# A planned attention-and-convolution layer on one core: fewer dummy transpositions at the opening, and another computed order of work

## The chip, the cores and the metric

The kernel runs on one core of one Trainium2 chip. The metric is the device time of one execution in microseconds (us). A core has TensorE (PE in the profile; PEld is its loading of weights), VectorE (DVE), ScalarE (ACT), GpSimd (POOL) and SyncE (SP). SP and POOL here issue DMAs; each of the engines works through its own list of instructions in order, so an instruction that waits holds back everything behind it on that engine.

## The reference

One decoder layer on x of 1024 tokens by 1024 channels. The numbers in brackets are column ranges of one input projection of 5632 columns.

```python
h = rmsnorm(x, norm_g)
proj = einsum('bsd,de->bse', h, w_in)                     # 1024 x 5632
q, k, v, a_gate, c_val, c_glu, c_gate = split(proj)       # 1024, 256, 256, 1024, 1024, 1024, 1024
y_att  = attention_branch(q, k, v, a_gate)     # 16 query heads, 4 key heads, three dilated windows
                                               # mixed by softmax denominators; times silu(a_gate)
y_conv = conv_branch(c_val, c_glu, c_gate, ...)  # val*sigmoid(glu), 31-tap causal convolution per
                                                 # channel, layernorm over channels, silu, silu(gate)
x = x + einsum('bse,ed->bsd', concat(y_att, y_conv), w_out)
return rmsnorm(x, final_norm_g)
```

## The kernel before

Nothing in this kernel is issued in the order in which it is written. The functions below `layer_kernel` only record operations in a list (`Plan.op`), each with an engine, an assumed cost, the buffers that it reads and writes, and a priority, which is its place in the list less the `boost` in force (`TUNE`). `Plan.order` (from L323) then plays the whole list through a clock for each engine. At each step it takes the operation that can start earliest, and of those that can start at once the one with the lowest priority number. The order found is the order of every engine's instructions. For an operation of SP or POOL, which is a DMA, the planned landing is the planned start plus 1.1 us, or the end of the DMA planned before if that is later, plus a time by size, plus 0.9 us (L397). What reads the data can't be planned earlier than that. `LIMITS` says how many buffers of a name may be held at once in the plan: three split weight tiles (`wh`, `wl`), two score tables (`tab`), five convolution inputs (`hc`), and so on. On the chip nothing of the planned times is left, only the order and the true dependencies.

Precision is kept by splitting a float32 operand into a rounded high part and a rest (`split_r`, `split_dma`); a product of two such operands takes three passes (high by high, high by low, low by high). A projection of 128 columns (`inproj`) is therefore 2 halves of 512 tokens x 8 blocks of channels x 3 = 48 matmuls of 128x512.

**The opening** (`prepare`). `pl.mm([...] * WARM)` records transpositions of a constant into a bank that nobody reads (tile `idle`). Then, for eight tiles of 128 tokens: load of `x`, sum of squares, scale (`stt` of x with `r` and with `gbc`, the norm gain spread over partitions by four matmul passes), transposition on TensorE (`xT`), split into `hhi` and `hlo`. Behind the first and the second token tile come `MORE[0]` and `MORE[1]` further dummy transpositions. `parameters` loads the convolution's weights and three vectors into the tile `rows` (the last is `in_ln_b`) and transposes them (`par_ps`).

**The sections.** `SECTIONS` lists which projections are recorded beside which pair of heads. A letter is a kind: h two projections for one convolution input, c a convolution gate, a an attention gate, q, k, v as usual. The number behind the list says how many `attend` go with it. So the first `attend` is in the section "h2 a0 q1", the third, attend(2), in "q3 h4", the last, attend(7), in "c4 c5". Each of the first eight sections also carries one `convolve`. An `attend` is scores on TensorE, a table added on VectorE, an exponential on ScalarE, transpositions back, and products with v.

**Behind the sections** come `load_wo_att` (load `raw_oa`, split into `woah` and `woal`, eight times), `layer_norm` for two halves (matmuls `mean`, `var`, `rb`), the attention part of the output projection (`att_part`: load `ya`, split, 24 matmuls `opsa` for each bank) and then the convolution part (`conv_part`: `yc`, matmuls `opsc`), which ends with the final norm and the stores. `outproj` loads the first `ya` only after the last `woal` has been written (the argument `after`).

Of the kernel before, what the change touches and what calls it, by code (L numbers as in the profile page):

```python
# [31 lines left out]

LIMITS = {"x": 5, "raw": 1, "raw_oc": 1, "raw_oa": 2, "wh": 3, "wl": 3, "tab": 2, "e": 7, "pt": 4, "vs": 4, "vc":
          4, "turn": 2, "opsa": 2, "score": 2, "hc": 5, "c": 7, "t": 1, "g": 1, "gl": 7, "y": 2, "ag": 4, "cc": 5,
          "qs": 5, "qf": 4, "kdh": 9, "kdl": 6, "yc": 2, "ya": 2, "zc": 7, "za": 3}

RESERVE = {"e": 7, "pt": 3}
BANKS = {"mm": 3, "sc": 2, "tp": 2, "o": 1}  # L40
WARM = 55
LATE = C_CG + 6 * P
MORE = (10, 12)
TUNE = {"w": 195, "use": 240, "ln": 65, "att": 240, "conv": 5, "wo": 215, "woa": -20, "ap": 0, "wait": 0.2116}
SECTIONS = [("k0 q0 h1 v", 0), ("h2 a0 q1", 1), ("h3 a1 q2 a2", 1), ("q3 h4", 1), ("h5 k1 a3 q4", 1), ("h6 a4 q5",
            1), ("c0 h7 a5 q6", 1), ("c1 q7 a6 a7 c2 c3", 1), ("c4 c5", 1), ("c6 c7", 0)]


def score_tables():
# [112 lines left out]
class Plan:  # L162
# [141 lines left out]
    def order(self):  # L304
# [20 lines left out]
        dma, table = 0.0, None  # L325
# [34 lines left out]
        while len(out) < n:  # L360
            best = None
            for e, todo in ready.items():
                now, pick = None, None
                for i in sorted(todo, key=self.prio.__getitem__):
                    t = start_of(i)
                    if t is None:
                        continue
                    soon = t - TUNE["wait"] if self.prio[i] < i - 300 else t
                    if now is None or soon < now - 1e-9:
                        now, pick, start = soon, i, t  # L370
                        if soon <= clock[e]:
                            break
                if pick is not None and (best is None or start < best[0]):
                    best = (start, pick)
            if best is None:
                raise RuntimeError(f"no slots: {oldest}, {inuse}, { {k: len(f) for k, f in free.items()} }, "
                                   f"{[(i, [b.name for b in ops[i][4]]) for r in ready.values() for i in sorted(r)[:3]]}")
            t, i = best
            e, cost, _, _, bufs = ops[i]
            if i in self.tables and self.tables[i] != table:  # L380
                table = self.tables[i]
                cost += 1.3
            ready[e].remove(i)
            for b in bufs:
                if not b.fixed and b not in held:
                    held.add(b)
                    if b.group:
                        inuse[b.group] = inuse.get(b.group, 0) + 1
                        taken[b.group] = taken.get(b.group, 0) + 1
                    b.slot = min(free[b.kind])[1]  # L390
                    free[b.kind].remove(min(free[b.kind]))
            end = t + cost
            clock[e] = end
            done = end + self.LATENCY
            if e in ("SP", "POOL"):
                dma = max(dma, t + 1.1) + self.dma_time[i]
                done = dma + 0.9  # L397
            elif e == "DVE":
                done = end + 0.13
            for b in bufs:  # L400
                if b.kind in PSUM_KINDS:
                    bank[b] = (e, done)
            same = {"PE": end, "ACT": end + 0.03}.get(e, done)
            for u in users[i]:
                at[u] = max(at[u], same if ops[u][0] == e else done)
                need[u] -= 1
                if not need[u]:
                    ready[ops[u][0]].append(u)
            for b in bufs:
                left[b] -= 1  # L410
                if not left[b] and not b.fixed:
                    free[b.kind].append((done, b.slot))
                    if b.group:
                        inuse[b.group] -= 1
            self.when[i] = t
            out.append(i)
            done_ops[i] = True
            while oldest < n and done_ops[oldest]:
                oldest += 1
# [44 lines left out]
def layer_kernel(tc, x, norm_g, w_in, conv_w, conv_b, ln_g, ln_b, w_out, fin_g, tab, out):  # L464
# [3 lines left out]
    def pool(name, space=None):  # L468
# [7 lines left out]
        **{k: (ps, k, BANKS[k]) for k in PSUM_KINDS},  # L476
    }, LIMITS)

# [34 lines left out]
    def c4(shape, name, dtype=F32):  # L513
        group = name.rstrip("0123456789_")
        return pl.buf("c4", shape, dtype, name, group=group if group in pl.limits else None)

    def bank(kind, name, group=None):
        return pl.buf(kind, [P, 512], F32, name, group=group)
# [12 lines left out]
    def split_r(hi, lo, src):  # L531

        pl.act(hi, src, AF.Copy)
        pl.tt(lo, src, hi.cast(F32), ALU.subtract)
# [12 lines left out]
    idle = bank("o", "idle")  # L547
    pl.mm([(idle[:, 0:P], ident, ident, None, None)] * WARM)
    rows = c4([P, D], "rows")
# [6 lines left out]
    def prepare(half):  # L556
# [12 lines left out]
        for j in range(4):  # L569
# [18 lines left out]
            for cg in range(2):  # L588
# [5 lines left out]
                split_r(hhi[half][:, 4 * cg:4 * cg + 4, o:o + P], hlo[half][:, 4 * cg:4 * cg + 4, o:o + P], b.split(P))  # L594
            if tb < len(MORE):
                pl.mm([(idle[:, 0:P], ident, ident, None, None)] * MORE[tb])
            for k in sorted(first_w) if tb == 1 else ():
# [25 lines left out]
    def load_raw(col):  # L623
        raw = c4([P, ND, P], f"raw{col}")
        pl.load(raw, w_in[:, col:col + P].rearrange("(c p) n -> p c n", p=P))
        return raw

    def split_w(col, raw, split=split_dma):
        wh, wl = c4([P, ND, P], f"wh{col}", F32R), c4([P, ND, P], f"wl{col}", F32R)
        split(wh, wl, raw)  # L630
        return wh, wl

    def load_w(col):
        if col in ready:
            return ready[col]
        old, pl.boost = pl.boost, TUNE["w"]
        w = split_w(col, load_raw(col), split_r if col >= LATE else split_dma)
# [3 lines left out]
    def inproj(col, use, cuts=((0, 512), (0, 512))):  # L641
        wh, wl = load_w(col)
        for half in range(2):
            b = bank("mm", f"ps{col}_{half}")
            for n0, n1 in zip(cuts[half], cuts[half][1:]):
# [5 lines left out]
                for c in range(0, ND, 2):  # L651
                    pl.mm([(b[:, n0:n1], wl[:, c + i, :], hhi[half][:, c + i, n0:n1], False, c + i == ND - 1)
                           for i in range(2)])
            pl.boost = TUNE["use"]
            use(half, b, slice(half * 512, half * 512 + 512))
# [448 lines left out]
    def boosted(name, gen):  # L1104
        while True:
            pl.boost = TUNE[name]
            w = next(gen, None)
            pl.boost = 0
            if w is None:
                return  # L1110
            yield w

    def section(k, weight, spine, more=()):
        nonlocal done
        proj, m = SECTIONS[k]
        hs = [boosted("att", attend(i)) for i in range(done, done + m)]
# [48 lines left out]
```

## Time and profile before

| | us |
|---|---|
| median of 3 runs | 899.86 (898.11 to 900.07) |
| the profiled execution, its own time | 898.14 |
| span of the profiled execution, first to last instruction | 896.3 |
| TensorE busy | 873.2 |
| VectorE busy | 655.8 |
| ScalarE busy | 592.8 |

The span lacks 1.84 us of the execution's own time, which lie around it. A busy TensorE is not one at its peak, since matmuls overlap in the profile: a 128x512 matmul is shown with some 0.39 us and starts 0.23 us behind the one before it. So idle time, the granted clock and the starts tell more than the busy share.

### The profile page before, as it was taken

How to read it: one execution, taken by the hardware profiler on the slowest of the kernel's cores; microseconds unless marked ns; L12 is line 12 of the kernel's file. 1: busy time of each engine (PE TensorE's matmuls, PEld its weight loads, DVE VectorE, ACT ScalarE, POOL GpSimd, SP SyncE). 2: the span in 40 equal slices, each digit the busy share in tenths (PEclk: the TensorE clock that was granted, in tenths of full speed). 3: DMA queues.
4: the chain of work that ended last, by engine and by line, in shares of the span. 5: the costliest groups of instructions: out<-in, count | busy, mean ns of one | idle time of the engine just before them, and what ended most of it. 6: DMA issues, size and time to landing. Idle time of an engine off the chain costs nothing.

```text
span 896.3 us, 13046 instructions
## 1 busy us (share of the span) xinstructions
PE 873.2 (97%) x4493; PEld 720.2 (80%) x4493; DVE 655.8 (73%) x1506; ACT 592.8 (66%) x1392; POOL 53.3 (6%) x69
## 2 busy tenths in 40 slices
PE   8999999999999999999999999999999799999996
PEld 7888888888888788887887887888787678878885
DVE  5769996689699689789989779943649895625333
ACT  4777368677958867977977947983896744414111
POOL 0001001010010010010010110101000000000000
PEclk9999999999999999999999999999999799999999
DMA  7533607254553474545355744455773697777111
GB/s 266 164 71 58 153 3 165 50 116 77 138 111 81 100 150 108 139 71 143 78 112 143 165 94 130 89 137 112 217 261 141 204 363 238 252 217 229 71 48 47
DMA packets 104953, 123.53 MB, mean 138 GB/s; under 512 B 17941, under 2 KB 78357, under 8 KB 104888
## 3 DMA queue, kind: packets, MB, share of 16 engines
q1 hardware_dynamic: 97000, 94.40, 34.3%
q0 software_dynamic: 7888, 28.32, 17.9%
q8 instruction: 35, 0.57, 0.3%
q14 instruction: 30, 0.25, 0.1%
HBM read 65.35 MB, written 24.84 MB: 101 GB/s over the span
## 4 chain that ended last, share of the span: by engine, by line
PE 86%; DMA 7%; DVE 3%; ACT 2%; issue 1%; SPq 1%; POOL 0%; DVEq 0%; ACTq 0%; POOLq 0%
PE ps L237 52%; PE opsc L237 10%; PE opsa L237 7%; PE sc_near L237 3%; PE on L237 3%; PE of L237 3%; PE sc_far L237 2%; DMA y<-comb 2%; PE tp_p L235 1%; PE tp_m L235 1%; DMA rows<-in_ln_b 1%; PE tp_s L235 1%; DMA raw_oc<-in_w_out 1%; ACT e L252 1%; DMA yc<-yc_dram 1%; DMA x<-in_x 1%
## 5 line engine op out<-in xcount | busy, mean ns | idle before, releaser
L237 PE MATMUL ps<-hhi,wh 128*128 128x512 f32 (+1 forms) x720 | 288.1, 401 | 0.3 <-ACT hhi L250 0.2
L237 PE MATMUL ps<-hlo,wh 128*128 128x512 f32 (+1 forms) x720 | 279.6, 390 | 0.3 <-DVE hlo L265 0.3
L237 PE MATMUL ps<-hhi,wl 128*128 128x512 f32 (+1 forms) x720 | 188.7, 395 | 0.0
L237 PEld LDWEIGHTS ps<-hhi,wh 128*128 128x128 f32 x720 | 135.6, 188 | 31.4 <-issue 0.5
L237 PEld LDWEIGHTS ps<-hlo,wh 128*128 128x128 f32 x720 | 135.8, 189 | 27.6 <-DVE hlo L265 0.8
L237 PEld LDWEIGHTS ps<-hhi,wl 128*128 128x128 f32 x720 | 129.3, 188 | 27.9
L252 ACT ACTIVATE e<-e,near 128x256 f32<-128x256 f32 (+1 forms) x256 | 115.6, 488 | 22.2 <-DVE near L265 12.3
L269 DVE SCALAR_TENSOR_TENSOR c<-hc,taps,c 128x511 f32<-128x511 f32 (+14 forms) x120 | 88.4, 737 | 0.3
L269 DVE SCALAR_TENSOR_TENSOR c<-t,taps,c 128x511 f32<-128x511 f32 (+14 forms) x120 | 88.6, 738 | 0.0
L269 DVE SCALAR_TENSOR_TENSOR t<-hc,taps,t 128x511 f32<-128x511 f32 (+6 forms) x112 | 82.5, 736 | 0.8 <-ACT t L252 0.8
L237 PE MATMUL opsc<-woc,yhc 128*128 128x512 f32 (+1 forms) x272 | 80.8, 381 | 0.0
L252 ACT ACTIVATE e<-e,far 128x224 f32<-128x224 f32 (+1 forms) x128 | 54.0, 424 | 36.0 <-DVE far L284 35.7
L298 POOL DMA_DIRECT2D wl<-raw x40 | 34.7, 868 | 452.1 <-ACT wl L252 350.1
L237 PEld LDWEIGHTS opsc<-woc,yhc 128*128 128x128 f32 x272 | 50.2, 188 | 10.6
L252 ACT ACTIVATE fjunk<-zc 128x512 bf16<-128x512 f32 (+1 forms) x17 | 10.3, 606 | 68.0 <-DVE zc L265 67.8
L237 PE MATMUL opsc<-woc,ylc 128*128 128x512 f32 (+1 forms) x136 | 52.0, 382 | 1.5 <-DVE ylc L265 1.5
L284 DVE CUSTOM_DVE_ANT_0 e<-sc_near,tab 128x256 f32<-128x256 f32 (+1 forms) x128 | 45.0, 404 | 9.9 <-PE sc_near L237 9.2
L250 ACT CAST wh<-raw 128x1024 fp32r<-128x1024 f32 x44 | 46.0, 1044 | 1.6 <-DMA raw<-in_w_in 1.4
L237 PE MATMUL opsa<-woah,yla 128*128 128x512 f32 x112 | 45.5, 406 | 1.5 <-DVE yla L265 1.5
L237 PE MATMUL opsa<-woah,yha 128*128 128x512 f32 x112 | 45.4, 405 | 0.0
L237 PE MATMUL opsa<-woal,yha 128*128 128x512 f32 x112 | 45.0, 402 | 0.0
L252 ACT ACTIVATE e<-e,f 128x96 f32<-128x96 f32 (+1 forms) x128 | 44.5, 439 | 0.2 <-DMA f<-back 0.2
(166 smaller groups left out, 1405.1 us busy)
## 6 DMA issues: line engine op xcount, KB each, us to landing
raw<-in_w_in SPq DMA_DIRECT2D x44, 512.0 KB, 4.5
wl<-raw POOLq DMA_DIRECT2D x40, 512.0 KB, 4.9
x<-in_x SPq DMA_DIRECT2D x8, 512.0 KB, 8.5
tab<-in_tab SPq DMA_DIRECT2D x8, 512.0 KB, 3.4
c_dram<-c SPq DMA_DIRECT2D x8, 512.0 KB, 3.3
g_dram<-g SPq DMA_DIRECT2D x8, 512.0 KB, 2.8
raw_oa<-in_w_out SPq DMA_DIRECT2D x8, 512.0 KB, 5.7
raw_oc<-in_w_out SPq DMA_DIRECT2D x8, 512.0 KB, 7.4
```

The lines of the kernel that those rows point to most:

```text
L235: nc.tensor.transpose(out.ap(), a.ap(), b.ap())
L237: nc.tensor.matmul(out.ap(), a.ap(), b.ap(), start=start, stop=stop)
L250: nc.scalar.copy(out.ap(), x.ap())
L252: nc.scalar.activation(out.ap(), x.ap(), func, **{k: ap_of(v) for k, v in kw.items()})
L269: lambda: self.nc.vector.scalar_tensor_tensor(out.ap(), a.ap(), ap_of(s), b.ap(), op0, op1),
L284: lambda: self.nc.vector.tensor_tensor_reduce(out.ap(), a.ap(), b.ap(), 1.0, ap_of(first), ALU.add, ALU.min, least.ap()),
L298: self.op("POOL", 1.0, lambda: self.nc.gpsimd.dma_start(ap_of(dst), x.ap(), accum_op=ALU.add), [dst], [x, dst])
```

## The change

The order of all instructions is computed anew, from these edits:

- 26 dummy transpositions in place of 55 at the start; 8 and 8 in place of 10 and 12 behind the first two token tiles.
- The planner takes every DMA's landing to be 1.0 us later (1.9 in place of 0.9).
- Limits: `wh` 4 (was 3), `hc` 7 (5), `qs` 6 (5), `zc` 8 (7); `tab` 1 (2), `cc` 4 (5), `kdl` 5 (6), `yc` 1 (2).
- Boosts: weight loads 215 (195), evictions of projections 120 (240), convolution -105 (5), output weights for the convolution part 155 (215), for the attention part -240 (-20), attention output 20 (0).
- Sections: the projection a2 goes from the section of attend(1) to that of attend(2); c3 goes from the section of attend(6) to that of attend(7); some are listed in another order.

No operation is added, and only dummy transpositions are taken away (29 + 2 + 4 = 35).

```diff
-LIMITS = {"x": 5, "raw": 1, "raw_oc": 1, "raw_oa": 2, "wh": 3, "wl": 3, "tab": 2, "e": 7, "pt": 4, "vs": 4, "vc":
-          4, "turn": 2, "opsa": 2, "score": 2, "hc": 5, "c": 7, "t": 1, "g": 1, "gl": 7, "y": 2, "ag": 4, "cc": 5,
-          "qs": 5, "qf": 4, "kdh": 9, "kdl": 6, "yc": 2, "ya": 2, "zc": 7, "za": 3}
+LIMITS = {"x": 5, "raw": 1, "raw_oc": 1, "raw_oa": 2, "wh": 4, "wl": 3, "tab": 1, "e": 7, "pt": 4, "vs": 4, "vc":
+          4, "turn": 2, "opsa": 2, "score": 2, "hc": 7, "c": 7, "t": 1, "g": 1, "gl": 7, "y": 2, "ag": 4, "cc": 4,
+          "qs": 6, "qf": 4, "kdh": 9, "kdl": 5, "yc": 1, "ya": 2, "zc": 8, "za": 3}
...
-WARM = 55
+WARM = 26
 LATE = C_CG + 6 * P
-MORE = (10, 12)
-TUNE = {"w": 195, "use": 240, "ln": 65, "att": 240, "conv": 5, "wo": 215, "woa": -20, "ap": 0, "wait": 0.2116}
-SECTIONS = [("k0 q0 h1 v", 0), ("h2 a0 q1", 1), ("h3 a1 q2 a2", 1), ("q3 h4", 1), ("h5 k1 a3 q4", 1), ("h6 a4 q5",
-            1), ("c0 h7 a5 q6", 1), ("c1 q7 a6 a7 c2 c3", 1), ("c4 c5", 1), ("c6 c7", 0)]
+MORE = (8, 8)
+TUNE = {"w": 215, "use": 120, "ln": 65, "att": 240, "conv": -105, "wo": 155, "woa": -240, "ap": 20, "wait": 0.2116}
+SECTIONS = [("k0 q0 h1 v", 0), ("h2 a0 q1", 1), ("h3 a1 q2", 1), ("a2 q3 h4", 1), ("h5 k1 a3 q4", 1), ("h6 a4 q5",
+            1), ("c0 h7 a5 q6", 1), ("a6 c1 a7 q7 c2", 1), ("c5 c4 c3", 1), ("c6 c7", 0)]
...
                 dma = max(dma, t + 1.1) + self.dma_time[i]
-                done = dma + 0.9
+                done = dma + 1.9
```

## Rows read from the trace of the kernel before

**Rows 1.** The page's first part: busy time, share and instructions of each engine.

```profile
PE 873.2 (97%) x4493; PEld 720.2 (80%) x4493; DVE 655.8 (73%) x1506; ACT 592.8 (66%) x1392; POOL 53.3 (6%) x69
```

**Rows 2.** Stretches: from:to, length, busy PE, PEld, DVE, ACT, POOL, clock, DMA, GB/s.

```profile
0.00:24.20 24.20, 19.91 (x138) 17.44 (x138) 13.02 (x29) 12.29 (x22) 1.02 (x8) 0.97 0.79 264
24.20:296.00 271.80, 271.80 (x1432) 225.89 (x1433) 225.05 (x534) 196.93 (x478) 20.66 (x24) 1.00 0.44 98
296.00:317.00 21.00, 18.91 (x114) 15.72 (x114) 13.18 (x32) 19.73 (x54) 0.88 (x1) 1.00 0.39 101
692.90:704.30 11.40, 4.96 (x21) 3.37 (x19) 9.21 (x18) 7.72 (x11) 0.00 (x0) 0.75 0.81 261
888.90:896.30 7.40, 0.02 (x1) 0.00 (x0) 1.98 (x7) 1.44 (x4) 0.00 (x0) 0.78 0.19 72
```

**Rows 3.** TensorE's waits: who waited for whom: total us, times, longest.

```profile
PE rb L237 <- DVE lst L269: 4.3, 1, 4.3
PE par_ps L235 <- DMA rows<-in_ln_b: 1.7, 1, 1.7
```

**Rows 4.** Order of time, TensorE, opening: start, us, what, count [idle before <-releaser].

```profile
1.45 8.23 PE L235 MATMUL idle<-ident 128*128 128x128 f32 x55 [1.45 <-POOL ident masks.py:199]
9.61 1.98 PE L237 MATMUL gbc<-gain,avg 1*128 1x512 f32 x4
11.52 1.31 PE L235 MATMUL idle<-ident 128*128 128x128 f32 x10
...
21.54 0.66 PE L235 MATMUL par_ps<-ident,rows 34*128 34x34 f32 x8 [1.70 <-DMA rows<-in_ln_b]
```

**Rows 5.** Order of time, VectorE, opening.

```profile
10.77 2.92 DVE L269 SCALAR_TENSOR_TENSOR x<-x,xst,gbc 128x512 f32<-128x512 f32 x4 [2.42 <-PE gbc L237]
```

**Rows 6.** Chain that ended last, opening: start, us, what.

```profile
9.87 11.42 DMA rows<-in_ln_b
```

**Rows 7.** Stretches of the opening, columns as in rows 2.

```profile
22.00:24.00 2.00, 1.62 (x12) 1.17 (x10) 0.57 (x1) 1.57 (x3) 0.00 (x0) 0.67 0.88 249
24.00:26.00 2.00, 1.82 (x9) 1.82 (x10) 2.00 (x5) 1.50 (x5) 0.00 (x0) 0.50 0.63 180
```

**Rows 8.** Chain, a stretch that TensorE makes alone: start, us, what, matmuls.

```profile
757.73 29.16 PE opsa L237 x126
```

**Rows 9.** Order of time, TensorE, the gap inside 296 to 317.

```profile
311.04 0.33 PE L235 MATMUL tp_w<-ident,e 128*128 128x128 f32 x1 [1.19 <-ACT e L252]
...
316.34 0.51 PE L237 MATMUL ps<-hhi,wh 128*128 128x512 f32 x1
```

**Rows 10.** Order of time, the passage from projections to the output projection: TensorE.

```profile
692.92 1.02 PE L237 MATMUL mean<-csum,avg 128*128 128x512 f32 x2
700.48 2.05 PE L237 MATMUL rb<-ident,lst 128*128 128x128 f32 x8 [4.28 <-DVE lst L269]
704.31 0.80 PE L237 MATMUL opsa<-woah,yla 128*128 128x512 f32 x1 [0.93 <-DVE yla L265]
```

**Rows 11.** The same passage on VectorE and on SP's queue.

```profile
696.31 1.22 DVE L265 TENSOR_TENSOR woal<-raw_oa,woah 128x1024 fp32r<-128x1024 f32 x1
703.17 1.09 DVE L265 TENSOR_TENSOR yla<-ya,yha 128x896 fp32r<-128x896 f32 x1
697.60 0.45 SPq L295 DMA_DIRECT2D ya<-y_dram  x1
```

**Rows 12.** A stretch of 20 us ahead of that passage, columns as in rows 2.

```profile
660.00:680.00 20.00, 20.00 (x118) 16.62 (x117) 13.83 (x22) 16.57 (x37) 0.00 (x0) 1.00 0.48 176
```

**Rows 13.** DMA issues: out<-in, queue, count, KB each, median us from issue to landing.

```profile
raw<-in_w_in SPq DMA_DIRECT2D x44, 512.0 KB, 4.5
raw_oc<-in_w_out SPq DMA_DIRECT2D x8, 512.0 KB, 7.4
ya<-y_dram SPq DMA_DIRECT2D x8, 448.0 KB, 7.9
yc<-yc_dram SPq DMA_DIRECT2D x8, 512.0 KB, 7.1
```

## The prediction

> **What bounds the kernel now.** I read the busy shares first, then the span cut into stretches, then TensorE's waits, then the order of time at each place where TensorE stood still. TensorE is busy 97% of the span [rows 1], VectorE and ScalarE about 70%. The stretches tell more [rows 2]: from 24.2 to 296 us TensorE has not one idle moment, at a clock of 1.00. What it loses lies in few places: 4.3 us idle of the first 24.2; 2.1 idle between 296 and 317; 6.4 idle of the 11.4 us from 692.9 to 704.3, with a clock of 0.75; and the last 7.4, in which it has nothing left to do. These are 20 of its 23 idle us (896.3 less 873.2). TensorE's longest wait, 4.3 us, is that of `rb`, layer norm's broadcast, for VectorE; next comes the parameters' transposition, 1.7 us for a DMA [rows 3]. The work of TensorE is the same before and after, dummies apart. So the change can gain where TensorE stands still or runs slow, and nowhere else; it can lose anywhere, since a new order can open a gap inside the 272 us that have none.
>
> **The opening, fewer dummies.** The 55 transpositions run from 1.45 to 9.68, 0.150 us each on average, and the four passes of `gbc` stand behind them [rows 4]. VectorE had the first scale factors at 8.35 and then waited 2.42 us for `gbc` [rows 5]. With 26, at 0.150 each, the dummies end at 5.4. Ten later ones took 1.31 us, 0.13 each [rows 4]; if all 26 ran at half that speed, 0.26 each, they end at 8.2. Both lie ahead of 8.35. `gbc` takes 1.98 us and its first half serves the first operation on VectorE, so VectorE starts at 8.35 to 9.2, that is 1.6 to 2.4 us earlier than at 10.77. No row shows when the gain's DMA landed, only that it had by 9.61; if that is the bound, the shift is smaller, down to none. The six dummies taken from behind the token tiles are hidden by VectorE's scaling, which takes 2.92 us for the two tiles [rows 5]; they are put at nothing, and 6 x 0.13 = 0.8 if uncovered.
>
> What is late next decides how much survives. At 19.84 TensorE reached the parameters' transposition and stood until 21.54 for the load of `in_ln_b`, which took 11.42 us from 9.87 on [rows 4, 6]. Nothing in the change makes that load faster. If the order stays, TensorE only arrives there earlier and waits longer: gain zero. If the transposition falls behind the next token tiles, the gain is the 2.4, the 1.7 and the low clock that followed: 0.67 for two us and 0.50 for two [rows 7] lost 0.7 + 1.0. So the ends are 5.8 gained and 1.7 lost (a longer wait and once more such a spell of low clock). The planner moves the landing of x and of the parameters by the same 1.0 us, so their order may well stay; I take 1.5 gained, nearer to zero.
>
> On the clock: it fell to 0.50, the lower of its two levels (1.2 of 2.4 GHz), after TensorE had stood still from 19.84 to 21.54 [rows 4, 7]. The Trainium skill (TensorE: Matmul & The Clock Gate, Part 1) says that the low clock is the default and that only activity lifts it. That speaks against taking dummies away; it is worked out from rows as a rival below.
>
> **A projection moved beside attend(2).** A 128x512 matmul takes 29.16 / 126 = 0.2314 us [rows 8], so a projection of 48 is 11.1 us of TensorE. Between 309 and 316 TensorE had none left and ran at the pace of the softmax: it waited 1.19 us for ScalarE at 311, and the next projection began at 316.34 [rows 9], in a stretch with ScalarE busy 19.73 of 21 [rows 2]. That is attend(2), whose section has three projections' worth of columns; a2 makes it four, at the cost of the section before, which has no idle to 296. A fourth `wh` buffer also lets the weights be ready sooner. The gain is at most the 2.1 idle, at least 0; I take 1.8.
>
> **A projection moved beside attend(7), and the passage to the output projection.** After its last projection TensorE does `mean` at 692.9, waits 4.28 for `rb`, starts `opsa` at 704.3 and runs the first of them at a low clock [rows 2, 10]. The chain behind it: the last `woal` is written at 697.53, the load of `ya` leaves at 697.60, and `yla` is ready at 704.26 [rows 11]. So `opsa` hangs on the weight splits. With c3 moved, 11.1 us of TensorE work no longer stand ahead of attend(7), so attend(7) can begin and end some 11 us earlier, and its followers on ScalarE and VectorE with it. VectorE has room: 13.8 us busy of 20 from 660 to 680 [rows 12]. Against it stands the boost of the splits, which falls by 220 places. For no gap at all the last `woal` must be written about as early as `ya` (7.9 median [rows 13]) and its two splits (0.94 + 1.09, of which only the second has its row [rows 11]; the first is put at the same 1.1) take: 10 us ahead of the last projection's end at 693, that is at 683, 14 us earlier than now. Ends: 8 gained (6.4 idle, and for the clock 1.6 of the 11.4 x 0.25 = 2.9 that it lacks, since part of that fell into idle time anyway), 8 lost (the gap once more). I take 3 gained, the priority and the section pulling against each other.
>
> **Later landings.** The planner's old sum for a 512 KB load on SP is 1.1 + 1.75 + 0.9 = 3.75 us, the new one 4.75 (1.75 from the code's 300 KB per us). Measured: 4.5 for the 44 weight loads, 7.4 for `raw_oc`, 7.9 for `ya`, 7.1 for `yc` [rows 13]. So readers were planned too early, and stood at the head of an engine's list while others behind them could have run. The new assumption is nearer. The Trainium skill (DMA: Bandwidth & Descriptors, Anatomy of one DMA) gives a fixed cost of about 2 us plus the bytes at 436 GB/s, an estimate of 3.2 for 512 KB; by that the old planner was late enough and the edit does nothing. The trace has 4.5 and more. How much of TensorE's time this is can't be read: of its waits above 1 us one is for a DMA (1.7, counted above). I add no gain.
>
> **The other limits and boosts.** `yc` 1: a token tile of the last stage takes TensorE 48 x 0.2314 = 11.1 us, the load 7.1 and the two splits 2.2, so one buffer still keeps up, as long as no load exceeds 8.9. `conv` -105: the sums are first read by `mean` of half 0, in the passage; the last convolution is far ahead of it. `use` 120: a projection's bank waits longer for its eviction; three banks hold 3 x 5.6 us of work. `tab` 1: the next table is loaded after the last near score of the pair before. All of these cost nothing while TensorE has other work planned, and a gap of 1 or 2 us where not. I put 0.5 lost, between 0 and 2.
>
> **The sum.** 1.5 + 1.8 + 3.0 - 0.5 = 5.8 gained, from 898.14, the profiled execution's own time: 892.3. The median of the runs shown is 1.7 above that execution (899.86), so the forecast for the median is **894**. Its own range, with the ends that can go together, is 886 to 898. The end of 7.4 us stays: no edit touches what follows the last matmul.
>
> **The rivals.**
>
> *No change.* The opening's gain ends at the load of `in_ln_b`, the passage's gain is eaten by the lower priority, small new gaps eat a2's: 898 to 901.7 (899.86 less or more 0.2%). For it: the load is as long whatever TensorE does. Against: the 2.1 and 6.4 idle us have their work moved towards them.
>
> *Slower: the attention weights' splits come later.* One place, the passage at 693. The splits lose 220 places, so VectorE takes layer norm and softmax first; if the last `woal` is written later than its 697.5 now, every us goes to `opsa`. Doubled, the gap costs 6.4 more and about 1.6 for the clock, so 8; less the 3.3 of the first two gains it is 898.1 + 4.7 + 1.7 = 904.5. It decides from 3.3 us later than now. For it: SP loads `ya` only behind the last split. Against: VectorE's free time ahead of it, and 11 us of work less in front of attend(7).
>
> *Slower: a cold opening.* If the clock is still low when the real work begins, the 16 transpositions and 24 matmuls of 256 columns up to 19.84 take twice their 16 x 0.13 + 24 x 0.116 = 4.9 us (0.116 is half of 0.2314). Nothing gained otherwise, that is 904.8. For it: the spell at 22 to 26. Against: VectorE and the loads set the pace there. [...]
>
> *Much faster.* The passage closes entirely and the parameters fall behind the token tiles: 5.8 + 2.1 + 8 = 16 gained, 884.
>
> **How the numbers follow.** The forecast 0.45, no change 0.15, splits later 0.20, cold opening 0.08, much faster 0.12. About 0.2% (1.8 us) is what a measurement of this kernel can tell from no change. Faster is the forecast and the much faster case, 0.57; the same 0.15; slower 0.28. The range reaches from 884 to 905.
>
> **What would show it.** In the profile after: `gbc` ends before 9.5 and VectorE's wait for it is gone; `par_ps` stands behind more `xT`; between attend(2)'s products there are `ps` matmuls and no wait for `e`; the stretch between the last `ps` and the steady run of `opsa` is shorter than 11.4 us with a higher clock. The prediction is wrong if new idle of over 3 us shows inside 30 to 680, or if the last `woal` stands nearer to the first `opsa`, or if the clock before 24 us is lower than 0.97.

## The result and the profile after

The kernel after takes 884.01 us (median of 4 runs, 883.21 to 886.12); the kernel before took 899.38 beside it (4 runs, 898.11 to 900.07). The ratio is 0.9834, with a 95% interval of 0.9813 to 0.9855: 15.4 us faster, where 5.9 had been forecast (899.86 to 894). The forecast's direction held; the size is that of the rival "much faster".

The profiled execution of after took 886.12 us, 2.1 above the median; its span is 884.3. Its page, first part (answers [rows 1]): TensorE has 4.9 us less busy time, 35 dummies less among it, and 98% of the span.

```profile
PE 868.3 (98%) x4458; PEld 719.8 (81%) x4458; DVE 656.1 (74%) x1506; ACT 591.9 (67%) x1392; POOL 53.3 (6%) x69
```

Stretches of after, columns as in [rows 2]. The gap of 296 to 317 is gone (21.00 of 21 busy; 18.91 before). The passage from the last projection to the output projection is 6.2 us long instead of 11.4, with 2.4 idle instead of 6.4 and the clock again at 0.75. The opening has less clock than before (0.81, and 0.59 up to 29.8). The end is 7.3, as good as unchanged.

```profile
0.00:24.20 24.20, 19.10 (x104) 16.27 (x105) 14.21 (x29) 12.95 (x23) 1.03 (x8) 0.81 0.79 263
24.20:29.80 5.60, 5.60 (x32) 5.60 (x31) 2.13 (x5) 4.25 (x9) 0.00 (x0) 0.59 0.91 262
296.00:317.00 21.00, 21.00 (x134) 18.45 (x133) 13.74 (x39) 20.39 (x56) 1.75 (x2) 1.00 0.38 95
317.00:687.90 370.90, 370.90 (x1965) 306.84 (x1963) 296.89 (x715) 286.52 (x708) 29.84 (x35) 1.00 0.56 136
687.90:694.10 6.20, 3.83 (x18) 3.03 (x19) 4.41 (x11) 6.06 (x8) 0.00 (x0) 0.75 0.90 286
877.00:884.30 7.30, 0.20 (x2) 0.00 (x0) 1.98 (x7) 1.43 (x4) 0.00 (x0) 0.85 0.19 72
```

TensorE's waits in after (answers [rows 3]): `rb` waits 2.4 instead of 4.3, and the parameters' transposition 3.0 instead of 1.7.

```profile
PE par_ps L235 <- DMA raw<-in_w_in: 3.0, 1, 3.0
PE rb L237 <- DVE lst L269: 2.4, 1, 2.4
```

**Lost time by stage.** Busy time hides slow matmuls, so for what follows I took, for each stretch, its length less the time that its matmuls take at the pace of an undisturbed stretch, each kind at its own (0.232 us for 128x512, half for 128x256, 0.109 for a transposition of 128x128), dummies left out. What is left is idle time, low clock and slow pace together. In both kernels some 840 us of the span are such work; the loss adds up to 56.0 before and 43.6 after, which agrees with the spans (12.0 apart) to 0.4 us. That is about the error of one entry.

| lost, us | 0 to 45 | 45 to last projection | of it 300 to 320 | passage, and output of attention | convolution's output and end | sum |
|---|---|---|---|---|---|---|
| before | 17.5 | 17.9 | 2.9 | 11.4 | 9.2 | 56.0 |
| after | 18.4 | 11.5 | 0.0 | 5.0 | 8.7 | 43.6 |
| gained | -0.9 | 6.4 | 2.9 | 6.4 | 0.5 | 12.4 |

Half of the gain is the passage, half lies in the 640 us of projections and attention: 2.9 of its 6.4 between 300 and 320, some 1.7 between 620 and 640, and no more than 0.6 in any other 20 us. The opening, which gives the change its name, gained nothing here.

**The opening of after**, order of time on TensorE and one row of VectorE (answers [rows 4, 5]). The forecast's first steps came out near: `gbc` starts at 7.84 instead of 9.61 (it ends at 9.82, not before 9.5), and VectorE starts to scale at 9.00 instead of 10.77, with 0.49 of its wait left. But all 42 dummies now stand in one row, since the planner put the 16 for the token tiles first as well; the forecast had counted 26 there. The projection begins at 12.78, and then TensorE stands 3.02 at the parameters' transposition. That wait is put down to a load of weights; the parameters' last row was issued at 10.98, behind the raw weights issued at 9.69.

```profile
1.45 6.46 PE L235 MATMUL idle<-ident 128*128 128x128 f32 x42 [1.45 <-POOL ident masks.py:199]
7.84 1.98 PE L237 MATMUL gbc<-gain,avg 1*128 1x512 f32 x4
...
12.78 0.58 PE L237 MATMUL ps<-hhi,wh 128*128 128x256 f32 x1
...
22.77 1.03 PE L235 MATMUL par_ps<-ident,rows 34*128 34x34 f32 x8 [3.02 <-DMA raw<-in_w_in]
9.00 2.92 DVE L269 SCALAR_TENSOR_TENSOR x<-x,xst,gbc 128x512 f32<-128x512 f32 x4 [0.49 <-PE gbc L237]
```

**The passage of after**, TensorE, VectorE and SP (answers [rows 10, 11]). The last `woal` ends at 686.6, ahead of the last projection's end; before it was written 4.4 us behind it. `var` stands right behind the last projection and waits for nothing.

```profile
687.73 0.95 PE L237 MATMUL var<-avg,ss 128*128 128x1 f32 x8
688.54 1.10 PE L237 MATMUL mean<-csum,avg 128*128 128x512 f32 x2
692.02 2.04 PE L237 MATMUL rb<-ident,lst 128*128 128x128 f32 x8 [2.38 <-DVE lst L269]
693.71 0.77 PE L237 MATMUL opsa<-woah,yha 128*128 128x512 f32 x1
684.26 2.35 DVE L265 TENSOR_TENSOR woal<-raw_oa,woah 128x1024 fp32r<-128x1024 f32 x2
685.55 0.99 SPq L295 DMA_DIRECT2D ya<-y_dram  x2
```

A few more rows of before, VectorE and then TensorE, show why it matters. Splits of `woal` and `woc` stood between VectorE's last sums of squares, so that `var` came 1.23 late, and again between its steps for `lst` (the `woal` of 696.31 is in [rows 11]), so that `rb` came 4.28 late.

```profile
692.01 0.68 DVE L265 TENSOR_TENSOR ss<-ss,sq 128x512 f32<-128x512 f32 x1
692.61 1.21 DVE L265 TENSOR_TENSOR woal<-raw_oa,woah 128x1024 fp32r<-128x1024 f32 x1
693.74 0.68 DVE L265 TENSOR_TENSOR woc<-raw_oc,woc 128x512 fp32r<-128x512 f32 x1
694.35 0.68 DVE L265 TENSOR_TENSOR ss<-ss,sq 128x512 f32<-128x512 f32 x1
...
696.23 0.16 DVE L275 TENSOR_SCALAR lst<-var 128x4 f32<-128x4 f32 x1 [0.61 <-PE var L237]
...
697.44 1.29 DVE L265 TENSOR_TENSOR woc<-raw_oc,woc 128x512 fp32r<-128x512 f32 x2
698.64 0.17 DVE L280 RECIPROCAL lst<-lst 128x4 f32<-128x4 f32 x1
695.17 1.02 PE L237 MATMUL var<-avg,ss 128*128 128x1 f32 x8 [1.23 <-DVE ss L265]
```

### The profile page after: what moved, and what is told of

Same layout as the page of the kernel before. It is cut to its first block, busy times and chain, and to the rows that moved or that the text cites. A ratio compares the mean times of both kernels' runs of the same rounds, so it can differ in the third digit from the quotient of the medians.

```text
span 884.3 us, 12947 instructions
## 1 busy us (share of the span) xinstructions
PE 868.3 (98%) x4458; PEld 719.8 (81%) x4458; DVE 656.1 (74%) x1506; ACT 591.9 (67%) x1392; POOL 53.3 (6%) x69
## 4 chain that ended last, share of the span: by engine, by line
PE 96%; DMA 2%; DVE 0%; ACT 0%; SPq 0%; issue 0%; ACTq 0%
PE ps L237 56%; PE opsa L237 10%; PE opsc L237 10%; PE sc_near L237 3%; PE on L237 3%; PE sc_far L237 3%; PE of L237 3%; PE tp_m L235 2%; PE tp_p L235 2%; DMA rows<-in_conv_w 2%; PE tp_s L235 1%; PE tp_w L235 1%; PE xT L235 1%; DMA raw<-in_w_in 1%; PE y L237 0%; SPq L295 0%
## 5 line engine op out<-in xcount | busy, mean ns | idle before, releaser
L237 PE MATMUL ps<-hhi,wl 128*128 128x512 f32 (+1 forms) x720 | 192.2, 397 | 0.0
L237 PEld LDWEIGHTS ps<-hhi,wh 128*128 128x128 f32 x720 | 137.5, 191 | 30.3 <-issue 0.5
L237 PEld LDWEIGHTS ps<-hlo,wh 128*128 128x128 f32 x720 | 137.7, 191 | 27.0 <-DVE hlo L265 0.7
L284 DVE CUSTOM_DVE_ANT_0 e<-sc_far,tab 128x224 f32<-128x224 f32 (+1 forms) x128 | 35.8, 318 | 12.8 <-PE sc_far L237 12.6
```

Source lines behind the costliest of these rows:

```text
L237: nc.tensor.matmul(out.ap(), a.ap(), b.ap(), start=start, stop=stop)
L284: lambda: self.nc.vector.tensor_tensor_reduce(out.ap(), a.ap(), b.ap(), 1.0, ap_of(first), ALU.add, ALU.min, least.ap()),
```

## The experiments

The change has five edits: the sections (a2 and c3 moved, some listed in another order), the limits, the boosts, the assumed landing and the counts of dummies. Each was done alone on the kernel before, and each was undone alone in the kernel after; the order is worked out anew in each. Then the sections were taken apart, one pair was tried, and the disputed opening was measured by itself. The kernel before ran beside them on each chip (medians 899.7 to 902.6), so the ratios are the better comparison; after's own is 0.9834.

### The five edits alone, on the kernel before

The sections:

```diff
-("h3 a1 q2 a2", 1), ("q3 h4", 1) ... ("c1 q7 a6 a7 c2 c3", 1), ("c4 c5", 1)
+("h3 a1 q2", 1), ("a2 q3 h4", 1) ... ("a6 c1 a7 q7 c2", 1), ("c5 c4 c3", 1)
```

> The kernel before with the new section list alone (a2 beside attend(2), c3 beside attend(7), two lists in another order). Theory A, the two moved projections bring most of the gain: the stretch 300 to 320 loses under 0.5 us of TensorE's time where it lost 2.9, the passage from the last projection to the output projection shortens from 11.4 us towards 6, and the time falls by 6 to 10 us, to 889 to 893. Theory B, the later landings bring it: within 2 us of before, 897 to 901. Theory C, the parts only work together: no gain or a loss, 899 to 905.

892.27 us, ratio 0.9895 (0.9864 to 0.9926): by the ratios 1.05 of the 1.66 per cent of the whole change, by the spans of the profiled executions 4.0 us of 12.0. The passage loses 6.4 us instead of 11.4, but the stretch from 45 us to the last projection still loses 17.6.

The landing:

```diff
-                done = dma + 0.9
+                done = dma + 1.9
```

> The kernel before with the planner's DMA landings 1.0 us later and nothing else. Theory A, the moved projections bring the gain: the gap at 300 to 320 and the passage stay, 898 to 901. Theory B, readers planned too early held up engines: the short waits between 40 and 690 go and the passage shortens, 888 to 894. Theory C, the parts only work together: 899 to 905.

903.5 us, ratio 1.0033 (1.0008 to 1.0058): slower. The passage itself got shorter: the last `woal` ends 0.4 us ahead of the last projection's end, and the first `opsa` starts 5.6 behind that end instead of 9.1. But a new wait of 7.5 us for `yla` stands in the output of attention, TensorE's row:

```profile
PE opsa L237 <- DVE yla L265: 8.4, 2, 7.5
```

The boosts:

```diff
-TUNE = {"w": 195, "use": 240, ..., "conv": 5, "wo": 215, "woa": -20, "ap": 0, ...}
+TUNE = {"w": 215, "use": 120, ..., "conv": -105, "wo": 155, "woa": -240, "ap": 20, ...}
```

> The kernel before with the new boosts alone (evictions 120, convolution -105, attention output weights -240 and the others). My prediction's slower rival: the splits of the attention output weights come later, the last of them after 697.5 us, the passage grows by 3 us or more, and the time is 900 to 906. Theory A: much the same, 898 to 902. Theory D, it is the boosts that clear the gaps: 888 to 894.

903.67 us, ratio 1.0038 (1.0012 to 1.0065): slower, from 7.9 us lost between 585 and 645, where before lost 2.8. The last `woal` starts at 701.4, 5.1 later than before, but the last projection ends 4.7 later as well, and the passage loses 11.6, as in before (11.4). So the lower boost of the splits, which the rival "splits come later" feared, cost next to nothing there.

The limits:

```diff
-LIMITS: "wh": 3, "tab": 2, "hc": 5, "cc": 5, "qs": 5, "kdl": 6, "yc": 2, "zc": 7
+LIMITS: "wh": 4, "tab": 1, "hc": 7, "cc": 4, "qs": 6, "kdl": 5, "yc": 1, "zc": 8
```

> The kernel before with the new limits alone (wh 4, hc 7, qs 6, zc 8; tab 1, cc 4, kdl 5, yc 1). Theory A: a fourth wh buffer shortens the gap at 300 to 320 at best by its 2.9 us, 896 to 900. If one buffer for yc or tab costs anything alone it shows in the last stage (89.0 us from the first to the last convolution output matmul) or ahead of the first scores of a pair: then 900 to 904. Theory D, the limits clear the gaps: 888 to 894.

901.31 us, ratio 1.0018 (0.9986 to 1.005): no difference that shows.

The dummies:

```diff
-WARM = 55, MORE = (10, 12)
+WARM = 26, MORE = (8, 8)
```

> The kernel before with the new counts of dummies, 26 and 8 and 8, and the order worked out anew with them; nothing else. The same 42 emitted in the old order gave 903.65 against 901.11 of before. The forecast's term: 898. The loads hold the opening: 899 to 902. A new order by chance: anything from 892 to 905, with the difference between 45 us and the last projection and not in the first 45.

899.14 us, ratio 0.9987 (0.9958 to 1.0016): no difference. TensorE lost 18.4 us of its first 45, against 17.5 before: what the opening was to give isn't there.

By their ratios the five alone come to -1.05, +0.33, +0.38, +0.18 and -0.13 per cent, together -0.3. All five at once gave -1.66. The parts don't add up.

### The five edits undone, in the kernel after

The diffs are those above, the other way round.

> The changed kernel with the old section list. Sections alone took 7 us from the kernel before, 5 of them in the passage. Theory A (the sections carry the change): the passage is back near 11 us and the time at 892 to 900. Theory C, the parts only work together: worse than before, 900 to 908.

902.72 us, ratio 1.0025 (1.0001 to 1.005): without the sections nothing of the gain is left. From 45 us to the last projection 27.7 us are lost, 11.0 of them between 400 and 420.

> The changed kernel with the old limits. Alone the new limits cost nothing that can be told from none. Theory A: 882 to 887. Theory C, the buffers are needed once more work stands beside a pair of heads (above all wh 4): 888 to 894, with gaps between 45 and 690.

893.68 us, ratio 0.992 (0.9891 to 0.9951): half of the gain is gone, and 7.0 us are lost between 460 and 480, where after loses 0.7.

> The changed kernel with the planner's landings 1.0 us earlier, as before. Alone the later landings cost the old kernel some 3 us, by 6 us more loss in the passage. Theory B, readers planned too early hold up engines wherever the sections are right: 887 to 893, with the loss spread between 45 and 690 us. Theory A: within 2 us of the changed kernel, 882 to 886.

887.66 us, ratio 0.9863 (0.9831 to 0.9895). Slower by some 3 us, within the two intervals. It is also the lower end of what theory B gave, and the loss lies where that theory put it: some 3.6 us more than in after from 45 us to the last projection, in no single place, against 2.5 less in the passage. So a small part for the later landing is neither shown nor ruled out. The weights' load that the forecast spoke of makes no wait of TensorE's here.

> The changed kernel with the old boosts. Alone the new boosts cost 4 us, 5 of them in two gaps near 300 and 600 us. Theory A: the changed kernel is as fast or faster without them, 880 to 886. Theory C, the boosts were right only for the new sections: 888 to 895, with a longer passage or gaps at 300 and 600.

884.83 us, ratio 0.9828 (0.979 to 0.9866): nothing.

> The kernel after with the old counts of dummies, 55 and 10 and 12, the order of all work worked out anew with them; the other edits stay. If the opening is held by the loads (the theory so far: 42 dummies placed otherwise and the parameters' loads moved earlier both changed nothing): 883 to 886. If the forecast's term for the opening is right: 885.5 plus or minus 1, some 1.5 slower than after. If the count matters through the order that the planner makes of it, as sections and limits without the new counts gave 902.8: over 890, with a gap between 400 and 490 us.

883.78 us, ratio 0.9806 (0.9753 to 0.986): nothing. With 77 dummies the clock is 1.00 all through the opening, where after with 42 runs at 0.50; rows of this kernel and then of after, 14 to 16 us:

```profile
14.00:16.00 2.00, 1.98 (x19) 1.74 (x16) 1.55 (x4) 1.29 (x3) 0.00 (x0) 1.00 0.68 170
```

```profile
14.00:16.00 2.00, 2.00 (x10) 2.00 (x11) 1.72 (x4) 1.90 (x5) 0.00 (x0) 0.50 0.80 199
```

Its projection starts 3.5 us later (16.32 instead of 12.78) and runs at full pace, and in the profiled execution it has lost 16.1 us of the first 45, 2.3 less than after. By the medians the two are the same. 0.50 is the lower of the clock's two levels, 1.2 of 2.4 GHz. The Trainium skill (TensorE: Matmul & The Clock Gate, Part 1) says that the low level is the default and activity releases it. These two rows do not show that: TensorE is busy 1.98 and 2.00 of the 2 us in them, and in after the clock had been 1.00 up to 10 us and fell while the `xT` ran, right behind `gbc`.

So in the kernel after the sections are worth 1.9%, the limits 0.9, and the other three nothing that these runs can tell. The forecast too had 4.8 of its 5.8 us on the two moved projections, but it priced them by the gaps at their places, and it put the limits at a loss.

### Which section, and which limit

Only a2 put back beside attend(1), in the kernel after:

```diff
-("h3 a1 q2", 1), ("a2 q3 h4", 1)
+("h3 a1 q2 a2", 1), ("q3 h4", 1)
```

> The changed kernel with a2 alone put back beside attend(1). All old sections cost it 19 us, in gaps between 345 and 470 us. Theory A as I predicted it: the stretch of attend(2) loses its 2 to 3 us again, 886 to 888. Theory E, the missing projection is felt at a later pair, since every pair behind it is one projection short: over 10 us, 894 to 902, with the gaps at 345 to 470.

905.79 us, ratio 1.0057 (1.0029 to 1.0084): the whole gain and more is gone. Stretches of this kernel, columns as above:

```profile
260.00:280.00 20.00, 18.37 (x90) 14.29 (x89) 17.93 (x57) 13.03 (x39) 2.96 (x4) 0.91 0.59 131
400.00:420.00 20.00, 14.38 (x81) 10.94 (x80) 19.28 (x71) 14.72 (x54) 2.48 (x3) 0.84 0.48 96
```

And the order of time on TensorE inside the second:

```profile
408.84 0.83 PE L237 MATMUL sc_far<-kdh,qf 128*128 128x224 f32 x4
409.60 0.48 PE L237 MATMUL sc_far<-kdl,qf 64*128 64x224 f32 x4
411.07 1.11 PE L237 MATMUL sc_near<-kdh,qs 128*128 128x128 f32 x4 [0.99 <-DVE far L284]
412.12 0.50 PE L237 MATMUL sc_near<-kdl,qs 64*128 64x128 f32 x4
413.66 1.32 PE L237 MATMUL sc_near<-kdh,qs 128*128 128x256 f32 x4 [1.05 <-DVE near L284]
```

There is no `ps` among them. TensorE has only scores and products left, most of them wait for a step on VectorE, and the clock falls to 0.84. VectorE is 19.28 of 20 busy there, but 18.32 in after at the same place, where TensorE has no idle moment; what differs is the `ps` between. Counted by lost time this stretch loses 10.5 us; after loses 0.4. One projection of 11.1 us, done a section earlier, is missing at 270 and again at 400. That alone doesn't make the gap, though: the kernel before has a2 in this same section and loses 0.7 us at 400. The gap comes of it together with the other new edits, and which of them is not shown.

The same move alone, on the kernel before:

```diff
-("h3 a1 q2 a2", 1), ("q3 h4", 1)
+("h3 a1 q2", 1), ("a2 q3 h4", 1)
```

> The kernel before, with a2 alone moved from the section of attend(1) to that of attend(2); all else as before. a2 carries the gain (taking it back from the kernel after cost 21.8 us): about 890, and the gap near 311 (rb and sc waits, 2.1 us idle) is closed. The gain needs the limits and later landings too: 897 to 901, and a gap somewhere else instead.

900.18 us, ratio 1.0003 (0.9975 to 1.003): nothing. It does what it was to do: 300 to 320 loses -0.1 instead of 2.9. But 320 to 340 now loses 1.7 (0.5 before), 400 to 420 1.4 (0.7), 520 to 560 2.5 (0.9), and the sum from 45 us to the last projection is 18.0 as against 17.9. The gap seems to be passed on.

Only c3 put back beside attend(6), in the kernel after:

```diff
-("a6 c1 a7 q7 c2", 1), ("c5 c4 c3", 1)
+("a6 c1 a7 q7 c2 c3", 1), ("c5 c4", 1)
```

> The changed kernel with c3 alone put back beside attend(6). As I predicted it: the passage to the output projection is longer by 3 to 8 us, 887 to 892. Theory F, the passage is shortened by something else (with all old sections it lost 4.0 us only): 883 to 886.

885.93 us, ratio 0.985 (0.9802 to 0.9899): no difference that shows, and the passage loses 5.7 as against 5.0. So in the kernel after c3 isn't what shortened the passage, though on the kernel before it was, or the new order of the lists that came with it: with all of the new sections the passage loses 6.4 there, with a2 alone 10.2.

The fourth `wh` buffer taken back, the other limits new:

```diff
-"wh": 4
+"wh": 3
```

> The kernel after with three wh buffers in place of four, the other limits new. If the fourth wh buffer is the limit that counted (projections' weights ready at 460 to 480, where the old limits lost 7 us): 890 to 894. If another limit (hc 7 in place of 5) did it: 883 to 886.

890.34 us, ratio 0.9877 (0.985 to 0.9904): by the ratios 0.4 of the 0.9% that all the limits are worth, by the medians 6.3 of 9.7 us. The loss sits in the same place as with all old limits: 5.8 us at 460 to 480. There the passes of a projection with `wh` are done, and its pass with `wl` comes only at 474.30, behind scores that wait for VectorE; after has passes of the next projection, with the fourth `wh`, between those scores:

```profile
468.65 1.12 PE L237 MATMUL sc_near<-kdh,qs 128*128 128x128 f32 x4 [0.80 <-DVE far L284]
469.70 0.49 PE L237 MATMUL sc_near<-kdl,qs 64*128 64x128 f32 x4
472.37 1.28 PE L237 MATMUL sc_near<-kdh,qs 128*128 128x256 f32 x4 [2.18 <-DVE near L284]
473.58 0.79 PE L237 MATMUL sc_near<-kdl,qs 64*128 64x256 f32 x4
474.30 2.07 PE L237 MATMUL ps<-hhi,wl 128*128 128x512 f32 x4
```

Sections and limits together, on the kernel before (their diffs above):

> The kernel before with the new sections and the new limits; landings, boosts and dummies as before. If sections and limits together are the whole of it: 884 to 887, TensorE losing about 11.5 us between 45 us and the last projection. If the later landings or the dummies are needed as well: 890 to 894, near the 892.3 that the sections gave alone.

902.82 us, ratio 1.0013 (0.9994 to 1.0033): both expectations failed. The limits, worth 0.9% in the kernel after, here cost 1.2 where the sections alone had gained 1.05. 12.5 us are lost between 400 and 500 (2.4 in before, 0.7 in after), where TensorE waits once for VectorE's `comb` and once for weights:

```profile
462.21 0.95 PE L237 MATMUL of<-pt,vc 96*128 96x256 f32 x6 [3.01 <-DVE comb L265]
482.53 2.11 PE L237 MATMUL ps<-hhi,wl 128*128 128x512 f32 x8 [3.13 <-DMA wl<-raw]
```

With the landing and the dummies added it is the kernel of 884.83 (old boosts); with boosts and dummies added that of 887.66 (early landing). And the kernel of 883.78 has landing and boosts without the dummies. So each pair of the three small edits serves as the third part; whether one of them alone would do wasn't tried. Nor was it tried how far the time moves when the order is worked out anew from an edit that has no reason to help, so part of each single result may be chance of the new order. The second row is the case that the forecast described under "later landings": an instruction planned too early stands at the head while its weights are on the way. Here it costs 3.1 us; the forecast had found no such wait in before, rightly, and drew from it that nothing could be gained.

### The opening by itself

The old order, but fewer of the dummies issued (26, 8 and 8; the edit of the first is shown); nothing is planned anew:

```diff
-pl.mm([(idle[:, 0:P], ident, ident, None, None)] * WARM)
+pl.mm([(idle[:, 0:P], ident, ident, None, None)] * WARM, emit=26)
```

> The kernel before in its own order, only that 26, 8 and 8 dummy transpositions are issued where 55, 10 and 12 were. By my prediction: the broadcast of the gain ends some 2.4 us sooner, the parameters' transposition then waits longer for its load, and the time is within 2 us of before, at best 3 us less: 896 to 900. Theory G, a cold opening: the granted clock is at its lower level in more of the first 30 us, 900 to 904.

903.65 us, ratio 1.0019 (0.9984 to 1.0055). `gbc` comes at 6.56, the projection at 13.06, and the parameters' transposition waits 4.7 us instead of 1.7. That is the forecast's own bound: TensorE arrives earlier and waits longer.

The kernel after's order with its 42 dummies, of which the last 16 are moved behind `gbc`, right ahead of the transpositions of the first two token tiles:

```diff
-pl.mm([(idle[:, 0:P], ident, ident, None, None)] * MORE[tb])
+pl.mm([(idle[:, 0:P], ident, ident, None, None)] * MORE[tb], emit=0)
-pl.mm([(b[:, ...], xt[:, ...], ident, None, None) ...])
+pl.mm([(b[:, ...], xt[:, ...], ident, None, None) ...], pre=[(idle[:, 0:P], ident, ident, None, None)] * 8)
```

> The changed kernel in its own order with the same 42 dummies, but 8 and 8 of them issued right ahead of the transpositions of the first two token tiles, behind the broadcast of the gain, where the kernel before had its 10 and 12; in the changed kernel all 42 come first. Theory G: the broadcast starts 1.7 us earlier, the clock stays at its upper level through the first projection (it was at 0.5 from 12 to 18 us), and the time falls by 1 to 3 us, to 881 to 883. If the load of the parameters sets the opening whatever the clock: within 1 us of the changed kernel, 883 to 885.

885.61 us, ratio 0.9842 (0.979 to 0.9894): nothing. The clock stays at 1.00 from 12 to 20, and the parameters' transposition waits 2.9 all the same.

The kernel after with the parameters' loads issued behind the gain's:

```diff
                 pl.load(gain, norm_g.rearrange("(o d) -> o d", o=1))
+                pl.load(rows[0:KT, :], conv_w)
+                for j, v in enumerate((conv_b, ln_g, ln_b)):
+                    pl.load(rows[KT + j:KT + j + 1, :], v.rearrange("(o d) -> o d", o=1))
```

> The kernel after with the four loads of the parameters' rows moved ahead of the load of the third token tile, behind that of the gain. If the opening is held by the load of in_ln_b, the 3.0 us wait of par_ps goes and with it the low clock at 22 to 28: 881 to 883. If TensorE would wait for the next load in the same place (raw weights, token tiles): 884 to 886.

886.75 us, ratio 0.9838 (0.9806 to 0.987): nothing gained. `par_ps` moves ahead of the projection and waits 5.06 there, now put down to the load of a token tile:

```profile
18.28 1.04 PE L235 MATMUL par_ps<-ident,rows 34*128 34x34 f32 x8 [5.06 <-DMA x<-in_x]
```

The transposition reads the parameters' rows alone, and their last one was issued at 8.56, among the token tiles; whether it had landed before that tile the profile doesn't tell. Between 14 and 18 us TensorE does nothing, with the projection behind the transposition in its list, while the loads move 346 and 301 GB/s. So an earlier place among the loads gains nothing. Lost in the first 45 us: 17.5 before, 18.4 after, 18.0 and 18.0 and 18.2 in these three kernels.

No kernel among these beats after by more than the intervals; the one with the old dummies equals it.

## Why the prediction was off

**The bridge.** 894.0 was 892.3 for a profiled execution and 1.7 more for the median. The profiled execution took 886.1, which is 6.2 less than that. The other 3.8 are the step from execution to median, and chance: after's median lies 2.1 below its profiled execution, where 1.7 above had been added. Its other three runs have a clock of 0.992 to 0.995, the profiled one 0.987. Of the 6.2, by the table, the stretch from 45 us to the last projection gave 5.1 more than forecast, the passage 3.4 and the end 0.5, and the opening 2.4 less; the sum is 6.6, within the error of the count.

| term | forecast, with its ends | measured by lost time |
|---|---|---|
| opening | 1.5 gained (-1.7 to 5.8) | -0.9 |
| a2 beside attend(2) | 1.8 (0 to 2.1) | 2.9 in 300 to 320 |
| limits and boosts; later landings | -0.5 (-2 to 0); none added | 3.5 in the rest of 45 to the last projection |
| passage | 3.0 (-8 to 8) | 6.4 |
| end | 0 | 0.5 |

**Right.** The passage and the gap of attend(2) were the places. The gap closed as described: the section brings TensorE a projection there. The passage got shorter, but still loses 5.0 us, at the clock of before (0.75), where a higher one had been named as a sign. `gbc` and VectorE moved by 1.8 us, within the expected 1.6 to 2.4; that is luck, since 42 dummies stand ahead of `gbc` and not 26. The rival "no change" described the opening, where the loads kept the gain. The rival "cold opening" had its clock too, 0.50 from 12 to 18 and 22 to 28, but not its price: TensorE waits for a load afterwards, at either clock. A clock under 0.97 before 24 us was also one of the signs that the prediction is wrong; it came (0.81), and the opening's gain is what did not come. The "splits later" rival fell: the last `woal` came 11 us earlier.

**The mis-sized terms.** First the passage: 3.0 was taken halfway, on the ground that the lower boost and the section pull against each other. They don't in the new setting. With the old boosts put back the kernel takes the same time, and the last `woal` is early. The chain shown above left the splits' place between the sums free, and 6.4 came of it, near the upper end of 8. That `opsa` hangs on these splits is borne out by all 20 kernels on record. In the six in which the last `woal` ends 4.4 to 4.8 us behind the last projection, the first `opsa` starts 9.0 to 9.7 behind it; in the other fourteen, where the split ends at most 0.3 behind, 1.2 to 5.8. On the kernel before, two edits bring that about alone, the sections (1.7 us ahead) and the later landing (0.4 ahead). That would explain why no edit undone alone in the kernel after brings the 11.4 back: the old sections lose 4.0 there, the old limits 5.1, c3 put back 5.7.

Then the rest of the 640 us. The forecast read 272 us without an idle moment as stretches with nothing to gain, and capped a2 at the 2.1 idle us of its own gap; less 0.5 for limits and boosts that made 1.3 for the whole stretch, and 6.4 were measured. The step that failed is this cap. The loss from 45 us to the last projection was 17.9 us, and only 2.9 of it idle time; the rest is slow pace, at a clock of 1.00. After loses 11.5 there, none of it idle, so 3.5 of the 6.4 gained had no idle time to show them. And where a projection is done changes it far from its place: putting a2 back beside attend(1) in the kernel after costs 10.5 us at 400, and moving it alone in the kernel before gains nothing. The edits' costs weren't terms of a sum. Limits that the forecast put at a loss of 0 to 2 are worth 9.7 us in the kernel after, nothing alone in the kernel before (1.0018, with 1 inside its interval), and cost some 10 us there beside the new sections. What in the planner makes one set of edits fit and another not stays open.

**The landings.** A 512 KB load was put at 4.5 us and more from rows, against the estimate of 3.2 from the Trainium skill (DMA: Bandwidth & Descriptors, Anatomy of one DMA), by which the old assumption would have been late enough and the edit worth nothing. The Trainium skill gives that fixed cost and rate there for DMAs that GpSimd issues; the 44 weight loads go out on SP's queue, so for them the forecast took the estimate further than it is meant. After has 4.7 for them in the median (DMA issues, columns as in [rows 13]) and 4.9 for the 40 `wl` of GpSimd:

```profile
raw<-in_w_in SPq DMA_DIRECT2D x44, 512.0 KB, 4.7
wl<-raw POOLq DMA_DIRECT2D x40, 512.0 KB, 4.9
```

Yet undoing the edit costs only 0.3%, inside the intervals, and doing it alone loses. The durations were on the rows' side, the time nearly on the side of nothing.

## What to carry to other kernels

Where a planner works out an order from lists and limits, price an edit to it by the work that the bounding engine has in hand at its later gaps too, not by the idle time at the place of the edit alone. A stretch with no idle time can still lose by slow pace: compare it with its work at undisturbed pace before saying that nothing can be gained there. And undo each edit in the finished kernel as well as doing it alone: here the two sets of runs disagree, and only the undoing tells what the finished kernel rests on. Where two edits each bring about the same thing, as the sections and the later landing did in the passage, undoing either shows nothing of it.

## What the runs showed of the hardware

The time of the kernel before follows its granted clock from run to run: 25 runs on one chip reach from 895.0 us at 0.994 to 905.8 at 0.985; a line through them has 12 us for 0.01. That is more than 0.01 of the 873 us that TensorE is busy (8.7). After and the kernels near it spread over 3 us at most, though in 4 runs each. What moves the clock between runs is not shown.

In after the clock was 0.50 for 12 us of the opening, and the kernels that kept 1.00 there, or part of it, have the same medians. For the first of its two spells the rows show why: TensorE then waits 3 us for a load, at either clock (3.0 in after, 2.9 with 16 dummies moved, where the clock was 1.00). For the second, behind that wait, they don't.
